# Moving two points in the order of a delta head: k's turning by two units of products, the scores by four units of gate products

## The chip, the cores and the metric

The kernel runs on one core of one Trainium2 chip. The metric is the time of one execution on the device in microseconds (us), as the median of several runs. One further execution was profiled, and all rows below are of that one.

## The reference

One layer of a hybrid model runs over 128 context tokens and 1024 noisy tokens. After a norm and a projection there are two branches, a retention with four heads and a gated delta rule with four heads, in both directions; then a gated merge, an output product and a feed-forward part. What matters here is the delta branch. For each head and each chunk of tokens:

```
dq, dk, dv = silu(short_conv(h @ w_in))           # dq, dk then l2-normalised
a_mat  = eye + strict_tril((dk*beta) @ dk.T * decay)
u, w   = solve(a_mat, dv*beta), solve(a_mat, dk*beta*exp(g))
scores = (dq @ dk.T) * decay
o      = (dq*exp(g)) @ S + scores @ (u - w @ S)
S      = S*exp(g_last) + (dk*exp(g_last - g)).T @ (u - w @ S)
```

Beside it the same projected input `h` is multiplied with gate weights (`C_DZ`, `C_RG`, `C_GD`, `C_GR`), which nothing in the delta heads waits for.

## The kernel before

The 1152 tokens lie in nine tiles of 128 and, for the projections, in three groups of 384 columns. A block of a projection makes 128 output columns for all tokens. Each fp32 product is made of three matmuls of split numbers (`mm3`, lines 147 to 150), so a block is 3 groups x 8 x 3 = 72 matmuls. `cm_units` hands a block out in 12 units of 6 matmuls, and the caller puts a unit wherever it wants one: `next(fill)` issues one unit of gate products.

A delta head goes through these steps:

- `Proj.keys`: the projections of k, q and v (`ps_cm`), the short convolution on VectorE (`conv`, tiles `y` and `s`), and the turning of k and q into token order (`token`: nine transposes into `ps_a` on TensorE, copies on ScalarE, sums of squares). `token_in(nm, fill, n)` issues n units of `fill` first.
- `Proj.values`: the same for the two halves of v. `token_in("v1", fill, 12)` puts one block of gate products ahead of the turning of v1.
- `head_decay`: decay factors on ScalarE and VectorE, then the scores: for each of nine tiles three matmuls into `ps_gq` (line 686), two tiles to a bank, from a pool of four banks that `ps_a` uses too. VectorE scales them into `LT` (lines 688 and 689) and `ST` (line 691).
- `solve_diag`: copies of `LT` into `c` (line 702, VectorE and ScalarE), a block transpose into `ld` (line 704), a matrix `md` set to the identity by GpSimd (lines 706 and 707), then 31 steps of substitution on VectorE (lines 722 and 725), and the results `c1` and `c2` (lines 727 and 729). The remaining units of the first `NF[h]` gate blocks are issued beside it.
- `solve_levels`: 32 x 32 and 64 x 64 products that put the blocks together. The first of them (`ps_y`, line 766) reads `c1` and `LT`. Between its stages stand two units of gate products each.
- `head_scan`: the recurrence over the chunks, then the next head.

The four heads are called head 0 to head 3 here; head 0 is `first` in the code. Each engine works through its own instructions in the order that the program fixes when it is built: the code's order, changed within limits by a scheduler, where `with behind(...)` forbids that an instruction is placed ahead of the marked one on its engine. `self.mark` is such a list. The weights of each gate block are split as they come in: a cast on ScalarE (`whi`, line 134), and a subtraction (`wlo`, line 135), which GpSimd does for gate blocks.

Of the kernel before, what the change touches and what calls it, by code (L numbers as in the profile page):

```python
# [46 lines left out]
def hybrid_layer(ctx: ExitStack, tc: tile.TileContext, I, O, dbg=None):  # L47
# [17 lines left out]
    def last(*engines):  # L65

        found, todo = [], set(engines)
        for i in reversed(nc.cur_bb.bb.instructions):
            e = str(i.engine).split(".")[-1]
            if e in todo:  # L70
                todo.discard(e)
                found.append(i)
                if not todo:
                    break
        return found

    def behind(*engines, marks=None):

        st = ExitStack()
        for i in marks or last(*engines):  # L80
            st.enter_context(tc.issue_after(i))
        return st
# [349 lines left out]
    def gate_units(fp, c0, dst, b, silu):  # L432

        def evac(g, ps):
            t_ = fp.tile([P, G], F32, tag="g_t", name="g_t")
            S.activation(out=t_, in_=ps, func=AF.Tanh, scale=0.5)
            if silu:
                V.scalar_tensor_tensor(out=t_, in0=t_, scalar=1.0, in1=ps, op0=ALU.add, op1=ALU.mult)
            nc.scalar.dma_start(out=dst[b, :, g * G:(g + 1) * G], in_=t_)
        yield from cm_units([("in", c0 + b * P, evac)], hT)  # L440
# [56 lines left out]
    def gate_sums():  # L497
        ps = pxt("ps_g")
        pv = ps[:, 0:2 * NT * 8].rearrange("p (a t c) -> p a t c", a=2, c=8)
        T.matmul(pv[:, 0, :, 0:4], triU, la[:, :, 0:4], start=True, stop=True)  # L500
        T.matmul(pv[:, 0, :, 4:8], triL, la[:, :, 4:8], start=True, stop=True)
        T.matmul(pv[:, 1], ones, la, start=True, stop=True)
        V.tensor_copy(out=gcol, in_=pv[:, 0])
        pt = pxt("ps_gt")
        T.transpose(pt[0:NT * 8, 0:P], gcol.rearrange("p t c -> p (t c)"), ident)
        gr = fp.tile([NT * 8, P], F32, tag="g_t", name="grow")
        V.tensor_copy(out=gr, in_=pt[0:NT * 8, 0:P])
        nc.sync.dma_start(out=gr_rows, in_=gr)
        S.activation(out=eg, in_=gcol, func=AF.Exp)
        V.tensor_scalar(out=neg, in0=eg, scalar1=-1.0, scalar2=None, op0=ALU.mult)  # L510
        S.activation(out=egl, in_=pv[:, 1], func=AF.Exp)
        V.tensor_tensor(out=ekl, in0=pv[:, 1], in1=gcol, op=ALU.subtract)
        S.activation(out=ekl, in_=ekl, func=AF.Exp)
# [10 lines left out]
    class Proj:  # L524
# [79 lines left out]
        def keys(self, first=False):  # L604

            self.conv("k")
            if not first:
                self.cm(["q"])
            self.chan("k")
            self.token_in("k", v0 := self.units(["v0"]), 0 if first else 4)  # L610
            self.conv("q")
            for _ in v0:
                pass
            if first:
                head_gates()
            self.chan("q")
            self.v1 = self.units(["v1"])
            self.token_in("q", self.v1, 0 if first else 2)
            self.mark = last("Activation")

        def values(self, fill, first=False):

            self.conv("v0")
            for _ in self.v1:
                pass
            if first:
                with behind("PE"):
                    gate_sums()
            if first:
                self.st["er"] = decay_rows(self.h)  # L630
            self.token("v0")
            self.conv("v1")
            self.token_in("v1", fill, 12)
            if first:
                for _ in range(10):
                    next(fill)
                self.mark += last("PE")

    def decay_rows(h):

        er = [dp.tile([P, NT, P], F32, tag="c", name="er", bufs=3) for _ in range(2)]
        for d in range(2):
            nc.sync.dma_start(out=er[d], in_=gr_rows.rearrange("(t c) x -> c t x", c=8)[d * 4 + h].partition_broadcast(P))
        return er
# [347 lines left out]
    for h in range(NH):  # L992
        st = pj.st
        fill = chain.from_iterable(gate_units(fp, *a) for a in per[h][:NF[h]])
# [6 lines left out]
        with behind("PE", "Activation"):  # L1001
# [6 lines left out]
            fill = chain.from_iterable(gate_units(fp, *a) for a in per[h][NF[h]:len(per[h]) - (NL if h == NH - 1 else 0)])  # L1008
# [1003 lines left out]
```

## Time and profile before

| what | value |
|---|---|
| median of 3 runs | 2349.46 us (2344.7 to 2349.5) |
| the profiled execution's own time | 2349.45 us |
| its span from first to last instruction | 2347.8 us |
| TensorE busy (PE) | 97% of the span |
| VectorE (DVE), ScalarE (ACT), GpSimd (POOL) busy | 64%, 40%, 29% |
| mean granted TensorE clock | 0.989 of full speed |

The profile gives for each instruction its start, its duration, and in brackets how long its engine was idle just before it and whom it waited for. An idle stretch of TensorE lengthens the kernel unless a later wait shrinks by as much; an idle stretch of another engine does so only where TensorE waits for its work.

### The profile page before, as it was taken

To read this page: it belongs to the slowest core of one execution; us is meant where nothing else is said; L and a number is where in the kernel's file an instruction comes from. 1 tells how busy PE (TensorE), PEld (TensorE's weight loads), DVE (VectorE), ACT (ScalarE), POOL (GpSimd) and SP (SyncE) were. 2 spreads that over 40 slices of the span, in tenths; PEclk is the share of its full clock that TensorE was granted. 3 is DMA by queue.
4 is the path that set the end of the run, shared out by engine and by line. 5 is a ranking of instruction groups with operands and counts; after the bars stand their busy time and mean duration, and the time that the engine had idled before them with its cause. 6 is when DMAs were issued, how large, how long until landed. Compare 5 with 4: busy or idle time off the path is not lost.

```text
span 2347.8 us, 38532 instructions
## 1 busy us (share of the span) xinstructions
PE 2270.4 (97%) x14315; PEld 2084.4 (89%) x14315; DVE 1496.0 (64%) x3263; ACT 943.2 (40%) x2000; POOL 670.5 (29%) x802
## 2 busy tenths in 40 slices
PE   7899999999999999999999999987999999999998
PEld 4899999899998989888889998777999999988887
DVE  5766868778667875466673443776666565564374
ACT  5434443533545353444541223664222222343333
POOL 2132332332323231344340110145443333300041
PEclk9999999999999999999999999998999999999999
DMA  8132233142333325112237965545542222285454
GB/s 261 29 94 77 64 73 74 50 89 80 63 73 55 88 42 166 43 43 62 94 130 255 298 217 172 184 142 157 150 125 82 85 73 69 65 305 185 126 190 133
DMA packets 272129, 279.70 MB, mean 119 GB/s; under 512 B 18578, under 2 KB 232516, under 8 KB 271172
## 3 DMA queue, kind: packets, MB, share of 16 engines
q1 hardware_dynamic: 230516, 226.33, 34.2%
q10 hardware_dynamic: 41264, 50.82, 6.3%
q8 instruction: 113, 1.85, 0.3%
q14 instruction: 76, 0.62, 0.1%
q0 software_dynamic: 160, 0.07, 0.0%
HBM read 214.26 MB, written 62.90 MB: 118 GB/s over the span
## 4 chain that ended last, share of the span: by engine, by line
PE 79%; DVE 6%; DMA 3%; issue 3%; ACT 3%; POOL 2%; ACTq 0%; POOLq 0%; DVEq 0%; SPq 0%
PE ps_f L148 10%; PE ps_f L150 10%; PE ps_f L149 10%; PE ps_cm L148 9%; PE ps_cm L150 9%; PE ps_cm L149 9%; PE ps_rp L148 2%; PE ps_rp L149 2%; PE ps_rp L150 2%; PE ps_m L148 1%; PE ps_m L149 1%; DMA gd_d<-g_s 1%; PE ps_m L150 1%; DMA g_s<-sz_d 1%; PE ps_ks L841 1%
## 5 line engine op out<-in xcount | busy, mean ns | idle before, releaser
L148 PE MATMUL ps_cm<-hTl,whi 128*128 128x384 f32 x1152 | 393.8, 342 | 4.6 <-DVE hTl L335 3.2
L149 PE MATMUL ps_cm<-hTh,whi 128*128 128x384 f32 x1152 | 388.1, 337 | 0.0
L150 PE MATMUL ps_cm<-hTh,wlo 128*128 128x384 f32 x1152 | 388.0, 337 | 0.0
L148 PE MATMUL ps_f<-bl,wc 128*128 128x288 f32 x776 | 233.9, 301 | 8.8 <-ACT wc L1655 7.6
L150 PE MATMUL ps_f<-bh,wc 128*128 128x288 f32 x776 | 231.7, 299 | 4.3 <-POOL wc L1656 4.3
L149 PE MATMUL ps_f<-bh,wc 128*128 128x288 f32 x776 | 232.2, 299 | 0.0
L148 PEld LDWEIGHTS ps_cm<-hTl,whi 128*128 128x128 f32 x1152 | 218.0, 189 | 10.1 <-DVE hTl L335 5.9
L135 POOL TENSOR_TENSOR wlo<-raw,whi 128x1024 fp32r<-128x1024 f32 x46 | 117.4, 2552 | 376.4 <-ACT whi L134 298.6
L149 PEld LDWEIGHTS ps_cm<-hTh,whi 128*128 128x128 f32 x1152 | 217.9, 189 | 0.0
L150 PEld LDWEIGHTS ps_cm<-hTh,wlo 128*128 128x128 f32 x1152 | 217.7, 189 | 0.0
L134 ACT CAST whi<-raw 128x1024 fp32r<-128x1024 f32 x88 | 92.3, 1049 | 179.2 <-PE ps_cm L149 136.9
L148 PEld LDWEIGHTS ps_f<-bl,wc 128*128 128x128 f32 x776 | 148.9, 192 | 9.5 <-ACT wc L1655 8.0
L150 PE MATMUL ps_f<-w2h,fl 128*128 128x512 f32 x396 | 154.1, 389 | 0.0
L149 PE MATMUL ps_f<-w2h,fh 128*128 128x512 f32 x396 | 154.1, 389 | 0.0
L148 PE MATMUL ps_f<-w2l,fh 128*128 128x512 f32 x396 | 154.0, 389 | 0.0
L150 PEld LDWEIGHTS ps_f<-bh,wc 128*128 128x128 f32 x776 | 149.3, 192 | 5.1 <-POOL wc L1656 4.9
L149 PEld LDWEIGHTS ps_f<-bh,wc 128*128 128x128 f32 x776 | 149.1, 192 | 0.0
L148 PE MATMUL ps_f<-bl,bh 128*128 128x288 f32 x456 | 135.1, 296 | 0.4 <-DVE u L1697 0.4
L150 PE MATMUL ps_f<-bh,bl 128*128 128x288 f32 x456 | 134.1, 294 | 0.0
L124 POOL TENSOR_TENSOR rsr<-msr,nhalf 128x1 f32<-128x1 f32 x36 | 22.2, 624 | 346.4 <-DVE sp L1905 177.2
L148 PE MATMUL ps_rp<-slo,hTh 128*128 128x512 f32 x288 | 119.5, 415 | 0.8 <-DVE slo L135 0.8
L150 PE MATMUL ps_rp<-shi,hTl 128*128 128x512 f32 x288 | 113.1, 393 | 0.0
(474 smaller groups left out, 5982.7 us busy)
## 6 DMA issues: line engine op xcount, KB each, us to landing
raw<-in_w_ffn_in SPq DMA_DIRECT2D x53, 512.0 KB, 4.2
raw<-in_w_in SPq DMA_DIRECT2D x48, 512.0 KB, 7.1
w2r<-in_w_ffn_out SPq DMA_DIRECT2D x82, 256.0 KB, 3.5
fr<-f_d SPq DMA_DIRECT2D x44, 384.0 KB, 4.3
wmq<-in_w_mod SPq DMA_DIRECT2D x32, 512.0 KB, 6.6
raw<-in_w_out SPq DMA_DIRECT2D x24, 512.0 KB, 4.1
wm<-in_w_mod SPq DMA_DIRECT2D x32, 256.0 KB, 6.1
f_d<-f_t ACTq DMA_DIRECT2D x44, 144.0 KB, 2.8
```

Source lines behind the costliest of these rows:

```text
L124: GP.tensor_tensor(out=out, in0=in_, in1=nhalf[:, 0:n], op=ALU.pow)
L134: S.copy(out=hi, in_=raw)
L135: (lo_eng or V).tensor_tensor(out=lo, in0=raw, in1=hi.bitcast(F32), op=ALU.subtract)
L148: T.matmul(ps, lh, rl, start=first, stop=False)
L149: T.matmul(ps, lh, rh, start=False, stop=False)
L150: T.matmul(ps, ll, rh, start=False, stop=last)
L841: T.matmul(ps, lh, r[0], start=first, stop=False)
```

## The change

```diff
@@ -607,7 +607,7 @@
             if not first:
                 self.cm(["q"])
             self.chan("k")
-            self.token_in("k", v0 := self.units(["v0"]), 0 if first else 4)
+            self.token_in("k", v0 := self.units(["v0"]), 0 if first else 6)
             self.conv("q")
             for _ in v0:
                 pass
@@ -631,10 +631,9 @@
             self.token("v0")
             self.conv("v1")
             self.token_in("v1", fill, 12)
-            if first:
-                for _ in range(10):
-                    next(fill)
-                self.mark += last("PE")
+            for _ in range(12 if first else 4):
+                next(fill)
+            self.mark += last("PE")
```

In heads 1 to 3, k is turned after six units of v0's projection, not four; the rest of that projection stands behind the turning. Behind the turning of v1, heads 1 to 3 now issue four units (24 matmuls) of gate products before the scores, where they had none, and head 0 issues twelve, where it had ten. The scores are held behind these by the mark on TensorE. No instruction is added to or taken from the work. After line 636 line numbers of the changed kernel are smaller by one.

On TensorE, at the scores of head 1 (`ps_a` is the turning of v1, `ps_cm` a gate product, `ps_gq` the scores), the order before was:

```order
L150 MATMUL ps_cm<-hTh_140,wlo 128x384
L574 MATMUL ps_a<-ident,s 128x128 x9
L686 MATMUL ps_gq<-kql,kqh 128x256
L686 MATMUL ps_gq<-kqh 128x256
L686 MATMUL ps_gq<-kqh,kql 128x256
...
L148 MATMUL ps_cm<-hTl_137,whi 128x384
```

and at the same place the changed kernel has 24 rows of `ps_cm` between the turning and the scores, of which the last three stand here:

```order
L148 MATMUL ps_cm<-hTl_137,whi 128x384
L149 MATMUL ps_cm<-hTh_136,whi 128x384
L150 MATMUL ps_cm<-hTh_136,wlo 128x384
L685 MATMUL ps_gq<-kql,kqh 128x256
L685 MATMUL ps_gq<-kqh 128x256
L685 MATMUL ps_gq<-kqh,kql 128x256
```

Before, 3 gate products lie among the 27 score matmuls and 213 more up to `ps_y`; in the changed kernel 24 lie ahead, 1 among them and 191 behind. The sum, 216, is the same. Heads 2 and 3 read alike; in head 0, 12 move from behind the scores to ahead of them.

On GpSimd, in the solve of head 1, the order before was (the two MEMSETs of `md` make the identity):

```order
L692 AFFINE_SELECT ST_3811<-ST_3811 128x1152
L693 AFFINE_SELECT ST_3812<-ST_3812 128x1152
L706 MEMSET md 128x1024
L707 MEMSET md 128x32
L135 TENSOR_TENSOR wlo<-raw,whi 128x1024 x2
```

and in the changed kernel, in heads 1 to 3 alike:

```order
L691 AFFINE_SELECT ST_3845<-ST_3845 128x1152
L692 AFFINE_SELECT ST_3846<-ST_3846 128x1152
L705 MEMSET md 128x1024
L135 TENSOR_TENSOR wlo<-raw,whi 128x1024
L706 MEMSET md 128x32
L135 TENSOR_TENSOR wlo<-raw,whi 128x1024
```

The subtraction of one gate block's weights has moved in between the two halves of the identity.

On VectorE, at the end of the substitution of head 3 (`g_t` is the silu of a gate block), the order before was:

```order
L725 TENSOR_TENSOR md<-md,tmp 128x16
L725 TENSOR_TENSOR md<-md,tmp 128x15
L727 STREAM_TRANSPOSE c_8875<-md 128x1024
L729 STREAM_TRANSPOSE c_8877<-md 128x1024
L438 SCALAR_TENSOR_TENSOR g_t<-g_t,ps_cm 128x384 x2
L770 COPY ysb<-ps_y 32x160
```

and in the changed kernel:

```order
L438 SCALAR_TENSOR_TENSOR g_t<-g_t,ps_cm 128x384
L721 TENSOR_TENSOR tmp<-ld,md 128x28
L724 TENSOR_TENSOR md<-md,tmp 128x2x16
L438 SCALAR_TENSOR_TENSOR g_t<-g_t,ps_cm 128x384
L724 TENSOR_TENSOR md<-md,tmp 128x2x14
...
L726 STREAM_TRANSPOSE c_8909<-md 128x1024
```

The two gate operations have moved from behind `c1` and `c2` into the last steps ahead of them.

## Rows read from the trace of the kernel before

**Rows 1.** The profile page: busy time of each engine, its share, and its instructions.

```profile
PE 2270.4 (97%) x14315; PEld 2084.4 (89%) x14315; DVE 1496.0 (64%) x3263; ACT 943.2 (40%) x2000; POOL 670.5 (29%) x802
```

**Rows 2.** TensorE in order of time (start, duration), around the scores.

```profile
147.46 0.36 PE L686 MATMUL ps_gq<-kql,kqh 128*128 128x256 f32 x1 [1.87 <-DVE ST L691]
...
347.24 0.39 PE L686 MATMUL ps_gq<-kql,kqh 128*128 128x256 f32 x1 [1.40 <-ACT v L577]
...
350.23 0.34 PE L148 MATMUL ps_cm<-hTl,whi 128*128 128x384 f32 x1
...
751.37 0.39 PE L686 MATMUL ps_gq<-kql,kqh 128*128 128x256 f32 x1 [1.96 <-ACT v L577]
```

**Rows 3.** VectorE in order of time, from first scaling to the copies of LT.

```profile
145.79 0.35 DVE L689 SCALAR_TENSOR_TENSOR LT<-LT,bk,ps_gq 128x128 f32<-128x128 f32 x1 [2.07 <-ACT LT L678]
...
345.71 0.35 DVE L688 SCALAR_TENSOR_TENSOR LT<-ST,bk,ps_gq 128x128 f32<-128x128 f32 x1 [2.21 <-PE ps_gq L686]
...
354.39 1.60 DVE L702 COPY c<-LT 32x576 f32<-32x576 f32 x1
...
547.40 0.35 DVE L688 SCALAR_TENSOR_TENSOR LT<-ST,bk,ps_gq 128x128 f32<-128x128 f32 x1 [3.80 <-PE ps_gq L686]
...
555.22 1.59 DVE L702 COPY c<-LT 32x576 f32<-32x576 f32 x1
...
749.28 0.35 DVE L688 SCALAR_TENSOR_TENSOR LT<-ST,bk,ps_gq 128x128 f32<-128x128 f32 x1 [2.24 <-PE ps_gq L686]
...
758.52 1.59 DVE L702 COPY c<-LT 32x576 f32<-32x576 f32 x1
```

**Rows 4.** VectorE in order of time: the making of c1 in heads 0 to 3.

```profile
183.84 2.08 DVE L727 STREAM_TRANSPOSE c<-md 128x1024 f32<-128x1024 f32 x1
...
384.42 2.07 DVE L727 STREAM_TRANSPOSE c<-md 128x1024 f32<-128x1024 f32 x1
...
585.21 2.08 DVE L727 STREAM_TRANSPOSE c<-md 128x1024 f32<-128x1024 f32 x1
...
788.75 2.08 DVE L727 STREAM_TRANSPOSE c<-md 128x1024 f32<-128x1024 f32 x1
```

**Rows 5.** TensorE in order of time: the first products of the levels, heads 0 to 3.

```profile
187.34 1.52 PE L766 MATMUL ps_y<-c,LT 32*32 32x32 f32 x36
...
387.25 1.52 PE L766 MATMUL ps_y<-c,LT 32*32 32x32 f32 x36
...
587.53 1.52 PE L766 MATMUL ps_y<-c,LT 32*32 32x32 f32 x36
...
791.39 1.52 PE L766 MATMUL ps_y<-c,LT 32*32 32x32 f32 x36
```

**Rows 6.** Head 1 in order of time: GpSimd, ScalarE and VectorE in the solve.

```profile
358.56 0.16 POOL L707 MEMSET md<- 128x32 f32 x1
...
362.27 1.05 ACT L134 CAST whi<-raw 128x1024 fp32r<-128x1024 f32 x1 [3.54 <-PE ps_cm L149]
...
363.40 2.65 DVE L722 TENSOR_TENSOR tmp<-ld,md 128x63 f32<-128x63 f32 x2
363.41 2.48 POOL L135 TENSOR_TENSOR wlo<-raw,whi 128x1024 fp32r<-128x1024 f32 x1 [4.68 <-ACT whi L134]
366.33 0.44 DVE L722 TENSOR_TENSOR tmp<-ld,md 128x60 f32<-128x60 f32 x2
```

**Rows 7.** VectorE in order of time: a gate operation of head 3.

```profile
791.87 0.52 DVE L438 SCALAR_TENSOR_TENSOR g_t<-g_t,ps_cm 128x384 f32<-128x384 f32 x1
```

**Rows 8.** TensorE after two idle stretches, in order of time.

```profile
720.22 2.18 PE L574 MATMUL ps_a<-ident,s 128*128 128x128 f32 x9 [2.69 <-DVE s L558]
...
1570.36 2.00 PE L1614 MATMUL ps_tr<-ident,xm 128*128 128x128 f32 x8 [3.31 <-ACT b L1625]
```

**Rows 9.** Windows behind these idle stretches: us, TensorE busy (instructions), granted clock, DMA share, GB/s.

```profile
720.20:723.00 2.80, 2.78 (x12) 0.51 0.00 0
...
1570.36:1576.00 5.64, 5.64 (x25) 0.50 0.61 193
```

## The prediction

> **What bounds the kernel now.** I read the busy shares first: TensorE works in 97% of the span [rows 1], so the time is its work plus its few waits, and every microsecond by which TensorE is held up in a delta head is still there at the end. Then I listed TensorE's waits in the heads, and read each place in order of time. At the scores it waits 1.87 us in head 0, 1.40 us in head 1 and 1.96 us in head 3, and not in head 2 [rows 2]: in head 0 for VectorE to free a bank, in the others for ScalarE's copies of v out of the banks that the scores want. The reader should then see a chain that shows as no wait at all. The scores feed VectorE's scaling; that feeds the copies, the substitution and `c1`; and `c1` feeds `ps_y` on TensorE, which meanwhile works off gate products. The end of `c1`, start plus duration, is at 185.92, 386.49, 587.29 and 790.83 us in heads 0 to 3 [rows 4]. TensorE arrives at `ps_y` at 187.34, 387.25, 587.53 and 791.39 us [rows 5]. So `c1` is ready just before it is wanted, with 1.42, 0.76, 0.24 and 0.56 us to spare. VectorE is idle at the start of that chain, because it waits for the scores: 2.21, 3.80 and 2.24 us in heads 1 to 3 [rows 3]. The chain starts when the scores start.
>
> **The change, k's turning.** It comes 12 matmuls later, and q's turning stays where it was. What VectorE does at that time is paced by its own queue, not by k's turning: in head 3 TensorE waits 2.69 us at q's turning for VectorE's `s` [rows 8]. A wait of TensorE at k's turning that goes would come back there. I cost this edit at nothing, from -0.3 to +0.3 us in each of three heads; its cover is VectorE's convolution of q, which stands ahead of k's squares.
>
> **The change, gains at the scores.** In head 1 gate products follow one another at (387.25 - 350.23) / 213 = 0.174 us, from the first behind the scores to `ps_y` [rows 2, 5]. So 24 of them take 4.17 us and 12 take 2.09 us. Each is more than the wait that stands there, and what is waited for does not move, so all three waits go: 1.87 + 1.40 + 1.96 = 5.2 us.
>
> **The change, what the solve loses.** The same 24 products no longer lie between the scores and `ps_y`.
> - Head 1: VectorE's first scaling moves from 345.71 to 349.88. The scaling of all nine tiles takes 555.22 - 547.40 = 7.82 us where it isn't interrupted, as in head 2 [rows 3]. The copies of `LT` begin at 357.70 instead of 354.39, 3.31 us late.
> - Head 2: there was no interruption, so the whole 4.17 us stays.
> - Head 3: 749.28 + 4.17 + 7.82 = 761.27 instead of 758.52, 2.75 us late.
> - Head 0: VectorE waited until 145.79 for a factor from ScalarE [rows 3], which doesn't move, and the scores move by 2.09 us only, to just about then. I take 0.1 us, between -0.5 and +0.6.
>
> Then GpSimd. In heads 1 to 3 the second half of the identity now waits behind a subtraction of weights. That subtraction waits for ScalarE's cast, which waits for TensorE to finish a block: 362.27 in head 1 [rows 6], 1.40 us earlier after the change. The subtraction began 1.14 us after the cast did, and takes 2.48: it ends at 364.49, and the identity is ready at 364.65 instead of 358.72, 5.93 us late. That is 2.6 us beyond the 3.31. But the same subtraction used to fall into the substitution, and one pair of steps took 2.65 us beside it, where a pair a little later took 0.44 [rows 6]: 2.2 us. That stall is now spent while VectorE waits for the identity. The difference is 0.4 us, part of which was slack; I take +0.2 us, between -2.2 (the identity is ready anyway) and +2.6 (a stall remains inside). Queued behind the identity on GpSimd is one more subtraction, for a gate block that TensorE comes to a block later; nobody waits for it at once. The Trainium skill has a rule on this, in "SBUF — State Buffer", "Who interferes with whom": an instruction of VectorE with two inputs in SBUF and one of GpSimd that reads SBUF exclude each other, and the one issued later waits for the whole of the other. By that rule the stall belongs to the overlap and goes with it, so the sum takes +0.2; if it belonged to the substitution itself, the sum would take +2.6 in each of three heads.
>
> In head 3 two gate operations also move ahead of `c1`, at 0.52 us each [rows 7]: +1.0 us. They are ready by then.
>
> So `c1` ends at 386.49 + 3.31 + 0.2 = 390.0 in head 1, 587.29 + 4.17 + 0.2 = 591.66 in head 2, 790.83 + 2.75 + 0.2 + 1.0 = 794.8 in head 3, each on that head's old clock. TensorE arrives at 385.85, 587.53 and 789.43, and now waits some 4.1, 4.1 and 5.4 us. Against the old starts of `ps_y` that is +2.7, +4.1 and +3.4 us; these already contain the gains of heads 1 and 3. Head 0 gives 0.1 - 1.87 = -1.8. What stands behind `ps_y` needs `c1` and `c2` in the same spacing as in head 2, where only 0.24 us were to spare and nothing waited. Sum: 2.7 + 4.1 + 3.4 - 1.8 = **+8.4 us**.
>
> **The clock.** A wait of some length costs twice. After 2.69 us of idling TensorE was granted 0.51 of full speed for 2.8 us, and after 3.31 us it had 0.50 for 5.64 us [rows 8, 9], that is 1.2 instead of 2.4 GHz; half of such a stretch is lost, 1.4 to 2.8 us. The three new waits are longer than either. The first 1.5 us behind them are 32 x 32 products, whose pace at the lower clock no row shows, so the cost lies between 0 and 2.8 us each; I take the shorter stretch's 1.4, **+4.2 us** in all.
>
> That makes 2349.45 + 8.4 + 4.2 = 2362.0 us from the profiled execution's own time, and the same from the median, 2349.46.
>
> **Does TensorE go around the wait?** All this needs that TensorE stands still at `ps_y` although gate products behind it are ready. In head 0 it stood idle for 1.87 us at a score [rows 2] with gate products behind it whose operands had long been there. The Trainium skill states in "TensorE: Matmul & The Clock Gate", "Part 2: What happens when you issue a matmul", that weight loads are pulled ahead of matmuls in flight, but that the matmuls themselves stay in program order. By that rule the sum is the one above; with matmuls that overtake, the gains of 5.2 us would stand alone, at 2344.2 us.
>
> **The rivals.** "No change" means within 0.2% of 2349.5, or 4.7 us: about what a measurement of this kernel can tell.
> - The waits at the scores go and nothing takes their place: 2344.2 us, faster. This needs `c1` to end no later than TensorE's new arrival, that is a chain shorter by 4.1 us in heads 1 and 2 and 5.4 in head 3; this stall and more of the same size would have to leave the chain, and the identity to wait for nothing. For it speaks only that one stall leaves; against it the slack of 0.24 to 0.76 us. It decides from slacks of 4 us on, which no row shows. With overtaking matmuls together: 0.07.
> - The identity is ready in time and the first stall is gone too: -2.4 us against my sum in each of heads 1 to 3, so +1.2 us, waits of 1.7 to 3.0 us, and clock losses of 0 to 1.4 us each: 2350.7 to 2354.9 us. The order of GpSimd's instructions speaks against it. 0.08.
> - A stall remains in the substitution: +2.4 us more in each of three heads and longer stretches at the lower clock, some 2369 to 2373 us. 0.09.
> - The forecast, waits of 4 to 5.5 us at `ps_y` in heads 1 to 3, with 0 to 8.4 us for the clock: 2357 to 2367 us. 0.76.
>
> **How the numbers follow.** The predicted time is 2362. Below 2353 lie the first rival and most of the second, above 2369 most of the third, together some 2 in 10: the range is 2353 to 2369. Slower by over 0.2% (above 2354.2) are the forecast, the third rival and a small part of the second: 0.86. Within 0.2% is most of the second: 0.07. Faster by more: 0.07.
>
> **What would show it.** Right: no wait of TensorE at `ps_gq`; waits of about 4, 4 and 5.5 us at `ps_y` in heads 1 to 3, released by VectorE's `c`; none or half a microsecond in head 0; the second half of the identity behind a `wlo` on GpSimd, and one long pair of steps in each substitution instead of two; a granted clock of 0.5 behind each wait. Wrong: `ps_y` without a wait, or with less than 2 us; or a scaling on VectorE that starts as early as before, because ScalarE or the banks set it rather than the scores.

## The result, and the profile after

The changed kernel takes 2361.69 us (median of 4 runs, 2359.12 to 2365.27) where the kernel before took 2347.76 us beside it: a ratio of 1.0056, with a 95% interval of 1.0042 to 1.0070, so 9.9 to 16.4 us slower. The profiled execution took 2359.28 us, its span is 2357.6 us, and the mean granted clock is 0.984 where it was 0.989. Line numbers behind line 636 are smaller by one than before.

TensorE's waits in the changed kernel, the first two rows (engine, what it waited for and on whom: us in total, times, the longest):

```profile
PE ps_y L765 <- DVE c L726: 12.5, 4, 4.8
PE ps_a L574 <- DVE s L558: 9.7, 6, 2.5
```

There is no row for `ps_gq` any more: the waits of [rows 2] at the scores are gone. In their place stand 12.5 us at `ps_y`, which had no wait in [rows 5]. TensorE in order of time at these places (start, duration; idle time before and its releaser in brackets):

```profile
185.38 1.51 PE L765 MATMUL ps_y<-c,LT 32*32 32x32 f32 x36 [0.17 <-DVE c L726]
388.03 1.58 PE L765 MATMUL ps_y<-c,LT 32*32 32x32 f32 x36 [3.75 <-DVE c L726]
593.30 1.58 PE L765 MATMUL ps_y<-c,LT 32*32 32x32 f32 x36 [3.78 <-DVE c L726]
800.85 1.58 PE L765 MATMUL ps_y<-c,LT 32*32 32x32 f32 x36 [4.76 <-DVE c L726]
```

Head 1 is followed back from there on VectorE, GpSimd and ScalarE, and head 3 on VectorE; the rows answer to [rows 3, 4, 6, 7]:

```profile
348.52 0.35 DVE L687 SCALAR_TENSOR_TENSOR LT<-ST,bk,ps_gq 128x128 f32<-128x128 f32 x1 [6.37 <-PE ps_gq L685]
358.95 1.50 POOL L705 MEMSET md<- 128x1024 f32 x1
359.22 1.05 ACT L134 CAST whi<-raw 128x1024 fp32r<-128x1024 f32 x1 [0.61 <-POOL ST L692]
359.65 1.25 DVE L703 STREAM_TRANSPOSE ld<-c 128x1024 f32<-128x1024 f32 x1
360.41 2.40 POOL L135 TENSOR_TENSOR wlo<-raw,whi 128x1024 fp32r<-128x1024 f32 x1
362.75 0.16 POOL L706 MEMSET md<- 128x32 f32 x1
362.94 0.27 DVE L721 TENSOR_TENSOR tmp<-ld,md 128x15 f32<-128x15 f32 x2 [2.04 <-POOL md L706]
...
372.83 2.38 POOL L135 TENSOR_TENSOR wlo<-raw,whi 128x1024 fp32r<-128x1024 f32 x1 [9.93 <-ACT whi L134]
372.96 2.54 DVE L721 TENSOR_TENSOR tmp<-ld,md 128x256 f32<-128x256 f32 x1
...
385.99 1.90 DVE L726 STREAM_TRANSPOSE c<-md 128x1024 f32<-128x1024 f32 x1
...
797.03 0.56 DVE L438 SCALAR_TENSOR_TENSOR g_t<-g_t,ps_cm 128x384 f32<-128x384 f32 x1
797.70 0.55 DVE L438 SCALAR_TENSOR_TENSOR g_t<-g_t,ps_cm 128x384 f32<-128x384 f32 x1
798.80 1.90 DVE L726 STREAM_TRANSPOSE c<-md 128x1024 f32<-128x1024 f32 x1
```

The reader sees the whole chain move. VectorE idles 6.37 us for the scores, and the identity waits behind GpSimd's subtraction. Before, two steps of head 1 were long, the pair of [rows 6] and this one:

```profile
375.93 2.69 DVE L725 TENSOR_TENSOR md<-md,tmp 128x176 f32<-128x176 f32 x2
```

Now one is left, at 372.96 us. From the first scaling to the start of `c1` it takes 385.99 - 348.52 = 37.47 us; in head 2 before, where nothing interrupted the scaling, it was 585.21 - 547.40 = 37.81 us. So the chain did not get longer, it started later.

Windows of the changed kernel behind the wait of head 1, and from `ps_y` of the first direction to `ps_y` of the second in the four heads (us, TensorE busy and instructions, granted clock, DMA share, GB/s):

```profile
388.03:390.00 1.97, 1.97 (x37) 0.50 0.00 0
390.00:392.00 2.00, 2.00 (x8) 0.50 0.04 8
392.00:394.00 2.00, 2.00 (x17) 0.59 0.00 0
394.00:396.00 2.00, 2.00 (x54) 1.00 0.00 0
...
185.38:199.99 14.61, 14.61 (x175) 1.00 0.19 50
388.03:404.55 16.52, 16.52 (x175) 0.83 0.23 35
593.30:609.62 16.32, 16.32 (x174) 0.84 0.18 16
800.85:817.35 16.50, 16.50 (x175) 0.82 0.24 59
```

The same work takes 14.61 us where TensorE came without idling, and 1.91, 1.71 and 1.89 us more behind the three waits: 5.5 us for the clock, at 1.2 instead of 2.4 GHz for some 5 us behind the wait shown.

### The profile page after: what moved, and what is told of

The parts are those of the page before. It is cut to its first block, busy times and chain, and to the rows that moved or that the text cites. A ratio compares the mean times of both kernels' runs of the same rounds, so it can differ in the third digit from the quotient of the medians.

```text
span 2357.6 us, 38532 instructions
## 1 busy us (share of the span) xinstructions
PE 2275.9 (97%) x14315; PEld 2090.5 (89%) x14315; DVE 1487.1 (63%) x3263; ACT 943.9 (40%) x2000; POOL 669.0 (28%) x802
```

## The experiments

Times are set against the kernel before on the same chip; "above" and "below" are ratio times that kernel's median, with the 95% interval. Within a trace I use one ledger, the sum of three entries: head 0 from its first turning to `ps_y`; the waits at the scores and at `ps_y` in heads 1 to 3; and what the stretch from `ps_y` to `ps_y` takes beyond 14.61 us. For the kernel before that is 104.17 + 3.36 + 0.44 us, for the changed one 102.47 + 12.29 + 5.51: 12.3 us more, beside 13.1 measured. The ledger shows where time goes in the heads, in one execution of each kernel. What lies outside it differs between executions too: the two profiled ones are 2359.28 and 2349.45 us long, 9.8 us apart.

**k's turning alone.** The kernel before, with k two units later:

```diff
-            self.token_in("k", v0 := self.units(["v0"]), 0 if first else 4)
+            self.token_in("k", v0 := self.units(["v0"]), 0 if first else 6)
```

> Only k's turning comes 12 matmuls later in heads 1 to 3; the scores stand where they stood before the change. My theory prices this edit at nothing: within 1 us of the kernel before (2347 to 2349 us), the waits at the scores still there (about 1.9, 1.4 and 2.0 us in heads 0, 1 and 3), and any wait that goes at k's turning back at q's turning. The rival, that the later turning of k holds up the squares and with them the convolution of q on VectorE, gives waits at q's turning that are 1 to 2 us longer in heads 1 to 3 and a time 3 to 6 us above the kernel before.

Measured: ratio 0.9998, 0.9987 to 1.0009. No cost of the edit is measured, within -3.0 and +2.1 us. Its profile has the waits at the scores of heads 1 and 3 still (1.43 and 1.84 us). In head 3 the wait of 0.31 us at k's turning is gone, and q's turning waits 3.87 us where it waited 2.69 [rows 8]. That is 1.2 us more, as the rival had it, but in this head alone.

**The scores alone.** The changed kernel, with k back at 4.

> Only the scores are moved (24 gate products later in heads 1 to 3, 12 in head 0); k's turning stands where it stood. My theory: the whole loss of the change is here, so 13 us above the kernel before and within 1.5 us of the changed kernel, with waits of 3.7 to 4.8 us at ps_y in heads 1 to 3. The rival, that k's turning has a share in the loss (the changed kernel waits 1.5 us at q's turning in head 2, where the kernel before waited 0.2): 2 to 5 us below the changed kernel, and no wait at q's turning in head 2.

Measured: ratio 1.0050, 1.0032 to 1.0068, so 11.7 us above, with waits of 3.76, 3.77 and 4.75 us at `ps_y`. The waits of the changed kernel are all here, and no share of k's turning is seen. The time alone, whose interval is 7.5 to 16.0 us, doesn't exclude a share of some us; the run before speaks against it.

**Head 0 alone.**

```diff
-            for _ in range(12 if first else 4):
-                next(fill)
-            self.mark += last("PE")
+            for _ in range(12 if first else 0):
+                next(fill)
+            if first:
+                self.mark += last("PE")
```

> Only head 0 is changed: its scores come 12 gate products later; heads 1 to 3 and k's turning are as before. My theory: the wait of 1.87 us at the scores goes and nothing takes its place, because VectorE's first scaling is set by a factor from ScalarE there and not by the scores: ps_y 1.8 us earlier, time about 1.8 us below the kernel before (2346 us), a difference at the edge of what can be measured. The rival, that head 0 loses as the other heads do: a wait of 1 us or more at ps_y of head 0 and a time equal to or above the kernel before.

Measured: ratio 1.0001, 0.9991 to 1.0011: the time doesn't decide, since 1.8 us lies inside. In the trace head 0 takes 102.44 us up to `ps_y`, 1.7 less than before, with 0.28 us of wait there, so the rival's wait of 1 us or more isn't there. But in the profile of k's turning alone, whose head 0 is that of the kernel before, head 0 took 103.83 us without the 1.87 us wait. There the granted clock was 0.50 from 102.1 to 105.4 us, where the two others have 1.00. The second run of the last version below, which has the edit, was granted 0.50 at the same place and took 103.85 us. So the edit gave 1.7 us where the clock stayed up in head 0 and nothing where it fell.

**The loss filled with work.** Products whose results nobody reads, where TensorE idles:

```diff
+        if h:
+            ps = pdt("ps_idle")
+            for i in range((20, 20, 24)[h - 1]):
+                T.matmul(ps[:, 0:G], hT[0][0][:, i % KT, 0:P], hT[1][0][:, i % KT], start=True, stop=True)
```

> The changed kernel with 20 more products (24 in head 3), whose results nobody reads, between the scores' gate products and ps_y in heads 1 to 3. They add 0.174 us each of work to TensorE, 11.1 us in all, which lies where TensorE stood idle. My theory, that the lower granted clock behind ps_y comes from the idling: the waits at ps_y fall to about 0.3, 0.3 and 0.6 us, ps_y starts as in the changed kernel, the clock behind it stays at 1.0, the 12 gate products behind it take 2.4 us again instead of 4.1, and the time is about 5 us below the changed kernel (2356 us). The rival, that the clock falls at ps_y for its small products themselves or that the slow products come of something else: 2.4 stays 4.1, and the time stays at the changed kernel's 2361 us. A third case, that the added products delay ps_y: a time above the changed kernel, up to 11 us.

Measured: ratio 1.0114, 1.0094 to 1.0133, 26.7 us above. None of the three cases: `ps_y` waits 0.44, 0.44 and 0.74 us, as the theory has it, but the second `ps_y` waits anew. VectorE and TensorE of this kernel in head 1, in order of time:

```profile
396.41 2.62 DVE L135 TENSOR_TENSOR lcv<-ST,hcv 128x1152 fp32r<-128x1152 f32 x1 [5.99 <-ACT hcv L134]
399.05 0.32 DVE L753 TENSOR_SCALAR MX<-ps_x 32x160 f32<-32x160 f32 x1
399.52 2.15 PE L792 MATMUL ps_y<-MX,LT 64*64 64x64 f32 x18 [3.83 <-DVE MX L753]
```

The added products had made the scheduler put the subtraction `lcv` ahead of `MX` on VectorE. As a test of the clock this run is void.

**The same, with VectorE's order held.** The split of the scores is issued behind the first level's second copy, where the changed kernel has it:

```diff
+                turn += 1
+                if turn == 3:
+                    marks.extend((last("DVE"), last("Activation")))
...
-                    split(*Shl[d], STs[d])
+                    with behind(marks=marks[0] + (marks[1] if d else [])) if h else ExitStack():
+                        split(*Shl[d], STs[d])
```

> The kernel with 20 more products (24 in head 3) ahead of ps_y again, with VectorE's and ScalarE's split of the scores held behind the first level, where the changed kernel has it (in the run before, VectorE's subtraction lcv had moved ahead of MX and TensorE waited 3.8, 3.8 and 2.3 us for MX). My theory: no wait at ps_y over 0.8 us nor at the second ps_y, a granted clock of 1.0 behind ps_y, 12 gate products in 2.4 us instead of 4.1, and a time about 5 us below the changed kernel, 8 to 9 above the kernel before. The rival, that what stands behind ps_y is paced by ScalarE's copies of c (done 6.2 us after ps_y's start in the changed kernel) and not by the clock: TensorE waits behind ps_y instead, and the time is within 1.5 us of the changed kernel.

Measured: ratio 1.0039, 1.0025 to 1.0054, 9.1 us above (5.9 to 12.7). That agrees with the theory, but the changed kernel wasn't beside it. The trace agrees in heads 1 and 2 only, with 14.62 and 14.61 us from `ps_y` to `ps_y`. Windows behind a stop of TensorE of 2.23 us in head 2, and from `ps_y` to `ps_y` in head 3, where TensorE waited 0.74 us:

```profile
614.73:621.10 6.37, 6.37 (x32) 0.50 0.47 72
800.50:816.68 16.18, 16.18 (x175) 0.89 0.25 62
```

Here the clock fell behind a wait of 0.74 us, and for longer behind the stop. Then the kernel and the changed one ran together:

> The changed kernel itself, beside the other three on the same chip: 12 to 14 us above the kernel before, with waits of 3.7 to 4.8 us at ps_y and 16.3 to 16.5 us from ps_y of the first direction to that of the second in heads 1 to 3, where head 0 has 14.6.

> The kernel filled2 again, beside the changed kernel on the same chip. My theory: with TensorE kept busy ahead of ps_y the 14.6 us from ps_y to ps_y come back in heads 1 and 2 at least, worth 1.7 to 1.9 us in each, so 3.5 to 5.5 us below the changed kernel. The rival: the time from ps_y to ps_y falls, but is given back at a later wait, and the two kernels' times are within 1.5 us.

Measured: 1.0050 (1.0038 to 1.0062) for the changed kernel, 1.0050 (1.0036 to 1.0064) for the filled one. The windows of the filled one, and TensorE in head 2:

```profile
386.33:400.95 14.62, 14.62 (x175) 1.00 0.22 35
588.22:602.84 14.62, 14.62 (x174) 1.00 0.12 25
796.37:810.98 14.61, 14.61 (x175) 1.00 0.23 59
...
613.52 0.80 PE L792 MATMUL ps_y<-MB,LT 64*64 64x64 f32 x11 [2.33 <-issue]
```

With TensorE busy ahead of `ps_y` the clock stays at 1.00 and all three stretches take 14.6 us; with the run before, five of six do, where the changed kernel had 16.1 to 16.6 us in each in both its profiles. So the slow stretch comes of the idling, though a wait as short as 0.74 us didn't rule it out. In head 2 TensorE stops for 2.33 us in the middle of 18 products, and its row names nobody that it waited for; this is the stop of 2.23 us in the run before. The DMA records point to its instructions: in both runs a packet of an instruction queue begins as the stop does (at 611.17 us for 611.19, and at 612.46 for 612.49), and since the packet before it TensorE had begun 517 and 519 matmuls and weight loads, where 255 are the mean. No experiment tested this.

By the ledger (with 11.6 us of added products and this stop) the kernel is 10.2 us above the one before, 2.1 below the changed one. The two intervals leave some 4 us either way between the two kernels, so neither this 2.1 nor the rival's nothing is excluded: 5.3 us come back at the place, and no gain is measured. The stop, and in the run before the slow clock behind it, are where some of it is given back. The profiled execution shows how far single ones differ: it took 2349.46 us, as little as the kernel before, at a mean granted clock of 0.993 for 0.989.

**A shorter chain.** The changed kernel without the last ten steps of the substitution:

```diff
-        for j in range(QD - 1):
+        for j in range(QD - 11):
```

> The changed kernel without the last 10 of the 31 steps of the substitution in every head, so that part of the diagonal blocks isn't solved: 5.9 us less of VectorE's work between the scores and c1 (380.10 to 385.99 us in head 1 of the changed kernel), more than the waits of 3.75, 3.77 and 4.76 us at ps_y. TensorE's instructions and their order are those of the changed kernel. My theory, that the loss is that chain and nothing else: no wait at ps_y, the clock stays up, the gains at the scores stand alone, and the time is about 5 us below the kernel before, 17 to 18 us below the changed kernel. The rival, that moving the scores costs something beside the chain (order of TensorE, banks, the gate products at the scores): a time at or above the kernel before although no wait at ps_y is left.

Measured: ratio 0.9974, 0.9965 to 0.9983, 6.1 us below the kernel before. Nothing waits at `ps_y`, and 14.63 us lie between the two `ps_y` in heads 1 to 3. So the later scores cost nothing that is seen beside this chain. The kernel before without these steps wasn't run; what the shorter work of VectorE gives elsewhere is in the 6.1 us too.

**Half the distance.**

```diff
-            for _ in range(12 if first else 4):
+            for _ in range(12 if first else 2):
```

> The changed kernel with two units (12 products) behind instead of four in heads 1 to 3; head 0 and k as in the changed kernel. My theory: every product moved back shortens a wait by 0.174 us, so ps_y waits some 1.7, 1.7 and 2.7 us in heads 1 to 3, 6.3 us less in all than in the changed kernel, no wait at the scores, and less of the clock is lost: 5 to 6.5 us above the kernel before. The rival, that a wait of any length brings the same loss of clock or that the chain is not moved in step with the products: waits as in the changed kernel and a time within 3 us of it.

Measured: ratio 1.0043, 1.0031 to 1.0055, 10.1 us above, more than expected. That is at most 3.0 us below the changed kernel (13.1 us above by the ratio of the result, 11.7 by the later one), as the rival had it. The waits, 2.52, 2.51 and 3.26 us, lie between the theory's (1.7, 1.7 and 2.7) and the changed kernel's. Head 1 on VectorE and TensorE, and the window from `ps_y` to `ps_y`:

```profile
357.63 1.25 DVE L703 STREAM_TRANSPOSE ld<-c 128x1024 f32<-128x1024 f32 x1 [0.64 <-ACT c L701]
359.86 2.53 DVE L721 TENSOR_TENSOR tmp<-ld,md 128x39 f32<-128x39 f32 x2
372.12 2.69 DVE L721 TENSOR_TENSOR tmp<-ld,md 128x240 f32<-128x240 f32 x2
386.33 1.52 PE L765 MATMUL ps_y<-c,LT 32*32 32x32 f32 x36 [2.52 <-DVE c L726]
...
386.33:402.13 15.80, 15.80 (x175) 0.89 0.23 33
```

The scores came 2.1 us earlier, `c1` only 1.2: VectorE now waits 0.64 us for ScalarE's copy, and both long steps are inside the substitution again. A wait of 2.5 us costs 1.2 us of clock where one of 3.75 cost 1.9. By the ledger it would be 6.5 us above, and the profiled execution of 2355.57 us is 6.1 above that of the kernel before. The 10.1 us are counted from a median of 2344.61 us, which is 4.8 us under the execution that the ledger starts from; so the difference of 3.6 us need not be time in this kernel.

**GpSimd's subtractions on VectorE.** The changed kernel, two gate blocks a head:

```diff
-    plan += [(("in", c0 + b * P), GP) for c0, _, b, _ in per[h]]
+    plan += [(("in", c0 + b * P), V if h and i in (3, 4) else GP) for i, (c0, _, b, _) in enumerate(per[h])]
```

> The changed kernel with the subtraction of two gate blocks' weights (wlo) on VectorE instead of GpSimd in heads 1 to 3: one stands behind ld's transpose, ahead of the substitution, and one inside it; GpSimd's identity then waits for no subtraction. My theory, that a long pair of steps (2.54 us where 0.45 to 0.5 is usual) is the overlap with GpSimd's subtraction and that the identity waits for one: no long pair in heads 1 to 3, the substitution begins about 0.9 us earlier, VectorE pays 1.1 us for the subtraction inside instead of 2.1, so c1 ends 1.9 us earlier against the scores; ps_y waits 1.9, 1.9 and 2.9 us, with the clock the time is 6 to 8 us below the changed kernel. The rival, that the long pairs belong to the substitution itself or to ScalarE's cast beside it: the long pairs stay, VectorE's two subtractions come on top, and the time is 3 us or more above the changed kernel.

Measured: ratio 1.0014, 1.0005 to 1.0023: 3.3 us above the kernel before, 9.4 below the changed one beside it. VectorE in head 1, TensorE in heads 1 to 3, and windows:

```profile
359.10 1.18 DVE L135 TENSOR_TENSOR wlo<-raw,whi 128x1024 fp32r<-128x1024 f32 x1
360.21 0.26 DVE L721 TENSOR_TENSOR tmp<-ld,md 128x15 f32<-128x15 f32 x2
370.23 0.42 DVE L721 TENSOR_TENSOR tmp<-ld,md 128x256 f32<-128x256 f32 x1
372.44 1.22 DVE L135 TENSOR_TENSOR wlo<-raw,whi 128x1024 fp32r<-128x1024 f32 x1
...
384.31 1.52 PE L765 MATMUL ps_y<-c,LT 32*32 32x32 f32 x36 [1.75 <-DVE c L726]
583.38 1.51 PE L765 MATMUL ps_y<-c,LT 32*32 32x32 f32 x36 [1.75 <-DVE c L726]
788.61 1.51 PE L765 MATMUL ps_y<-c,LT 32*32 32x32 f32 x36 [2.55 <-DVE c L726]
...
384.31:398.93 14.62, 14.62 (x174) 1.00 0.23 48
583.38:599.17 15.79, 15.79 (x175) 0.89 0.17 20
788.61:804.38 15.77, 15.77 (x174) 0.89 0.23 61
```

No step of heads 1 to 3 is long any more: the 128x256 step took 2.54 us beside GpSimd's subtraction and takes 0.42 without it. The chain is 2.0 us shorter, as expected, and the clock gives back more than expected (2.3 us lost instead of 5.5).

**A version meant to beat both.** The trace of before shows what holds up ScalarE's copies of v at the scores of heads 1 and 3: they stand behind a tanh that waits for the DMA that frees its buffer. ScalarE in head 1 of the kernel before:

```profile
346.22 0.49 ACT L436 ACTIVATE g_t<-ps_cm 128x384 f32<-128x384 f32 x1 [1.25 <-DMA td_d<-g_t]
346.61 0.58 ACT L577 COPY v<-ps_a 128x512 f32<-128x512 f32 x1
```

In this kernel the tanh of a gate block's last part is issued behind the copies, head 0 has its 12 products, and heads 1 to 3 have the scores where they were before:

```diff
         def evac(g, ps):
+            if hold and g == NG - 1:
+                held.append(lambda: out(g, ps))
+            else:
+                out(g, ps)
...
             self.token_in("v1", fill, 12)
+            while held:
+                held.pop()()
```

> A version meant to beat both kernels: heads 1 to 3 have the scores where the kernel before has them, head 0 has them 12 products later, and ScalarE copies v out of its banks ahead of the last tanh of the gate block beside it (which in the kernel before stands first and waits for the DMA that frees its buffer: 346.22 and 750.35 us). My theory: what the waits at the scores of heads 1 and 3 are released by is that tanh's place in ScalarE's order; they go (1.40 and 1.96 us) without delay of VectorE's chain, and with head 0's 1.8 us the time is 5 us below the kernel before (0.998). The rival, that the copies come too late for the banks anyway, or that the later tanh holds up a bank of the gate products: the waits are still 1 us or more, or come back at ps_cm, and the time is that of the kernel before less 1.8 us or more than that.

> The kernel late_tanh again, for its gain beside the others on the same chip. From its profile (waits of 1.4 and 2.0 us at the scores of heads 1 and 3 gone, head 0's gone for 0.2 at ps_y): 5 us below the kernel before; from its first timing 2.6 us, between 0.5 and 4.5. A kernel that is 1 us or less below would say that the rest is given back at the waits for VectorE's s at the turnings.

Measured: ratio 0.9989 (0.9981 to 0.9998), and the second time 0.9993 (0.9985 to 1.0002): 2.6 and 1.6 us below the kernel before. ScalarE at the scores of head 1, and TensorE behind `ps_y` in head 3, of the second run:

```profile
342.64 1.23 ACT L585 COPY v<-ps_a 128x512 f32<-128x512 f32 x3
343.82 0.49 ACT L444 ACTIVATE g_t<-ps_cm 128x384 f32<-128x384 f32 x1
...
784.71:801.60 16.89, 16.52 (x175) 0.90 0.20 59
```

No wait at the scores is left in any head, and `ps_y` waits 0.24 us at most. By the trace, what was expected beyond 1.6 us went in two places. Head 0 took 103.85 us in this execution (0.3 less than before, not 1.8), with the slow clock at 102 us told above. In head 3 VectorE's `ysb` stands behind gate operations, so that TensorE waits 0.37 us in the level; behind that it was granted 0.50 from 791.4 to 794.7 us, and the stretch lost 2.3 us in all. In the first run the two places gave 102.38 and 0.8 us. It is the fastest version here that does all the work, well below the changed kernel; against the kernel before its gain is at the edge of what was measured, and the second interval doesn't exclude that there is none.

## Why the prediction was right, by its steps

- **k's turning at nothing** holds as far as it was measured: 0.9998 for the edit alone, within -3.0 and +2.1 us, which is wider than the stated 0.3 us a head.
- **The waits at the scores go** (5.2 us): they do. The share of head 0 is less sure than its row made it look, 1.7 us or nothing, because the 1.87 us wait isn't there in an execution whose clock falls in head 0.
- **The chain moves with the scores.** Set on the run's own clock (v0's turning of head 1 is at 328.92 us after and was at 330.28 before, 1.36 us earlier), the prediction has the first scaling at 348.52 us, the identity ready at 363.29 and `c1` done at 388.64; measured are 348.52, 362.91 and 387.89. The waits at `ps_y` were to be 4.1, 4.1 and 5.4 us and are 3.75, 3.78 and 4.76. The net of waits is 12.46 - 5.23 = 7.2 us for the predicted 8.4.
- **The identity behind GpSimd's subtraction, and the stall that leaves.** I took +0.2 us for the two together; from the first scaling to `c1` it is -0.3. That the long step is the overlap with GpSimd is shown by moving the subtraction: 2.54 us became 0.42. The rule of the Trainium skill ("SBUF — State Buffer", "Who interferes with whom") says the same, that VectorE's work with two inputs in SBUF and GpSimd's reads of SBUF exclude each other. In head 1 the long step began 0.13 us after the subtraction and ended 0.29 us after it.
- **The two gate operations of head 3** stand ahead of `c1`, 0.56 and 0.55 us, for the predicted 1.0.
- **The clock.** 1.4 us a wait was taken, 4.2 in all; the stretches behind `ps_y` show 1.91, 1.71 and 1.89, 5.5 in all, inside the stated 0 to 8.4. The term was too small by 1.3 us because the 12 gate products behind the 32x32 products fall into the slow stretch whole, while the 32x32 products themselves hardly notice it (1.58 us for 1.51). That the idling is the cause is shown at the place by filling it, in five of six stretches; that the 5.5 us would come back in the kernel's time is not shown, since the filled kernel gave nothing measurable back.
- **TensorE doesn't go around a wait**: it idles for 4.76 us with gate products behind `ps_y`. That agrees with the Trainium skill ("TensorE: Matmul & The Clock Gate", "Part 2: What happens when you issue a matmul"), by which matmuls stay in program order.
- **The rivals.** The one on the faster side needed a chain shorter by 4 us and more; with 5.9 us cut off the time is 6.1 us below the kernel before, so that was the right condition, and it is not met. The one in the middle (the stall gone and the identity in time) was put at 2350.7 to 2354.9, 1.2 to 5.4 us above the profiled time of before; built on purpose, it measured 3.3 above. The one of 2369 us and more did not occur.

The terms erred in opposite directions, 1.2 us too much for the waits and 1.3 too little for the clock; that the total of 2362.0 came within 0.3 us of the median is partly luck, seen beside an interval of 6.5 us. The total was counted from 2349.46 us, and the kernel before took 2347.76 beside the changed one: as a difference, 12.6 us were predicted and 9.9 to 16.4 measured.

## What to carry to other kernels

Before work is moved ahead of a stage to cover a wait, look at what the stage starts on another engine and with how much slack that comes back: here three waits of 1.4 to 2 us were covered, and a chain with 0.2 to 0.8 us to spare became waits of 3.8 to 4.8 us. A wait is better taken away at what releases it: the copies of v behind a tanh that had no hurry, for 1.6 and 2.6 us here. And a wait of TensorE is to be costed with what it does to the clock behind it: the waits of 2.5 to 4.8 us at `ps_y` cost 1.2 to 3.4 us more here.

## What the runs showed of the hardware that I had not expected

- The price of a wait for the clock is not one number: behind 0.74 us of idling the stretch of 14.6 us took 14.61 once and 16.18 another time, behind 1.75 us 14.62 and 15.79, behind 2.5 us 15.8 to 15.9, behind 3.75 us 16.1 to 18.0 (the 18.0 with the scores alone, in head 2).
- The subtraction of 128x1024 takes 2.4 us on GpSimd and 1.2 on VectorE, and beside it VectorE's step loses 2.1 us: on VectorE it costs VectorE less than on GpSimd.
- TensorE stopped for 2.2 to 2.3 us inside a group of 18 products at the same place in both profiles of one kernel, with no releaser in its row. A packet of instructions began to move as the stop began, after twice the usual number of instructions; whether TensorE waited for it stays open. Behind the one stop the granted clock was 0.50 for over 6 us, behind the other 1.00.
